# One recurrence unit takes its second read-back from another ring of buffers, and the last attention unit prepares its last queries and gates at later steps

## The chip, the cores and the metric

The kernel runs on one core of one Trainium2 chip. The core has several engines that run side by side, each with its own queue of instructions: TensorE (PE in the profile) multiplies matrices, ScalarE (ACT) and VectorE (DVE) work element by element, GpSimd (POOL) does little here, and SyncE (SP) issues the transfers between the chip's memory and the buffers of the core. An engine works its queue from the front: an instruction that waits holds up what stands behind it. The metric is the time of one execution on the device in microseconds.

## The reference

The reference is one layer of an encoder over 2048 tokens of width 1024, in 32-bit floats. The tokens form a grid of 32 rows by 64 columns.

```python
mod = c_act @ ada_w[l] + ada_b[l]
shift, scale, gate = jnp.split(mod, 3, axis=-1)
h = (_layernorm(x) * (1.0 + scale[:, None, :]) + shift[:, None, :]).astype(x.dtype)
proj = h @ w_in[l]
q_h, i_h, zf_fw, zf_bw, g_h, q_n, k_n, v_n, g_n = jnp.split(proj, split_pts, axis=-1)
y_hg = _hgrn2_branch(q_h, i_h, zf_fw, zf_bw, g_h, lb_fw_all[l], lb_bw_all[l], hg_norm_g[l])
o_na = _neighbourhood_attention(na_heads(q_n), na_heads(k_n), na_heads(v_n), rpb[l])
...
y_na = o_na * jax.nn.silu(g_n)
y = jnp.concatenate([y_hg, y_na], axis=-1) @ w_out[l]
z = DEEPNORM_ALPHA * x + gate[:, None, :] * y
x = (_layernorm(z) * ln_g[l] + ln_b[l]).astype(x.dtype)
```

One projection of 1024 to 9216 columns feeds two branches. The first is a gated linear recurrence with 8 heads of 128, run forwards and backwards over the sequence in chunks of 32; the two directions are added, normalised by their root mean square and multiplied by a gate. The second is a neighbourhood attention with 16 heads of 64: each query sees a window of 8 rows by 16 columns around it, with a bias by relative position, and its output too is multiplied by a gate. Both outputs, 2048 columns together, go through one output projection, and the residual and a layer norm end the layer.

## The kernel before

Each product of 32-bit floats is made from three faster ones: an operand is split into a high part (a rounded copy, made on ACT) and a low part (what is left, a subtraction on DVE), and PE multiplies high by high, high by low and low by high. In the names, h and l at the end mark the parts: `wh` and `wl` of weights that come in as `wr`, `qh` and `ql`, `KA`/`KB` and `KL`, `yh` and `yl`.

The work goes in phases. The start makes the modulation, the normalised `h`, and the first projections, and runs the attention of the first half of the rows. Then come 16 units of the recurrence, 8 heads (`u` = 0 to 7) for the first half of the tokens and 8 for the second, woven with projection matmuls (the helper at L278, which the profile shows as `pj<-h,wh`). A border follows, in which the last recurrence unit drains while PE works on the value projection (`vproj`, L291, with the evacuation of its PSUM tiles on ACT at L299 and the store at L301). Then 8 units of neighbourhood attention for the second half, woven with further projections; the last of them is woven with the first 4 of 16 token tiles of the output projection (`out_stream`, matmuls at L1547 to L1549). A dense phase does the rest of the output projection.

PE runs its instructions in the order in which the program writes them. The orders of ACT, DVE, POOL and SP are set by a scheduler that simulates a timeline: what is ready earlier by its model, or has priority, comes first. A change in the program's text can so move an instruction on these engines, or leave it where it was.

Buffers are rings: `tl(tag)` takes the next buffer of the ring `tag`, and whoever writes it waits until the last reader of the tile that had it is done. Four rings matter here. `cl` has 4 buffers of 128 by 512 floats and `de` has 2 (both belong to the recurrence phase); `bk` has 4, and `vt` holds outputs and raw weights, both in the attention phase. Memory of a phase that has ended is used again by the next: the attention's tile `Z`, which POOL clears at L771 and L772, lies over buffers of the recurrence.

Of a recurrence unit of the second half, the function `hgrn_tail` (L622) does the end. The forward state of the first half goes into the second by three matmuls (L690) on the queries `qh` and `ql`, which were stored earlier and are read back (L683, L684), and their result is added (L691) to a partial output `o1`, read back at L685; `sg`, read back at L686, is the gate. This is done for two groups `g` of 512 tokens, one after the other. `rms_out` (L342) then squares on ACT (L345), splits on DVE (L347, L349), sums over the channels on PE (L354, L355), takes the root on ACT (L357, L358), multiplies on DVE (L359, and by the gate L361), and stores (L362). All four tiles of each group come from `cl`, so that the second group's tiles take the first group's buffers.

In the attention phase `Prep` makes what a unit's steps read: `k` and `q` split keys and queries (keys: ACT L992, DVE L994; queries: ACT L976 and L977, DVE L978 and L979), `gate` makes a gate tile (ACT L1010, L340, L341, DVE L339, L1012), `v` loads values, `table` loads biases. `prep_now` (L1140) says at which of a unit's steps these are written in the program. A step's scores go from PE (L1055 to L1062) to DVE (L1071, bias and row maximum), ACT (L1076, exponential), DVE (L1080 and L1081, division by the sum), PE (L1104, transposes), ACT or DVE (L1110, L1108, copies), and PE (L1126, times the values); DVE then multiplies by the gate (L1136). In the last unit `wo_load` (L1499) and `wo_split` (L1504) bring in and split weights of the output projection (load L1502, high part on ACT L1507, low part on DVE L1508), by steps written in a table `extra`, and `y_split` splits the inputs (ACT L1539, DVE L1540).

Of the kernel before, what the change touches and what calls it, by code (L numbers as in the profile page):

```python
# [11 lines left out]
F32R = mybir.dt.float32r  # L12
# [26 lines left out]
def body(ctx: ExitStack, tc: tile.TileContext, t):  # L39
# [48 lines left out]
    def nm(s):  # L88
        cnt[0] += 1
        return f"{s}_{cnt[0]}"  # L90

    def tl(tag, dt=F32, shape=None):
        if tag in cur["smap"]:
            tag = cur["smap"][tag]
            return sh.tile([P, 512], dt, tag=tag, name=nm(tag), bufs=SH[tag])
        return cur["pool"].tile([P, 512] if shape is None else shape, dt, tag=tag, name=nm(tag), bufs=cur["bufs"].get(tag, 1))
# [536 lines left out]
    def hgrn_tail(u, half, sgs, ubs, decs, qibs, os_, decb_all):  # L633
# [8 lines left out]
        for g in (1, 0):  # L642
# [20 lines left out]
            if half == 0:  # L663
                dma(op_d[u][:, tk], ob)
                dma(sg_d[u][:, tk], sgs[g])
                qb, qh, ql = tl("t"), tl("cl", F32R), tl("cl", F32R)
# [9 lines left out]
        if half == 1:  # L676
            Rh, Rl = tl("Sb", F32R, [P, P]), tl("Sb", F32R, [P, P])
            dve.tensor_copy(Rh, R)
            dve.tensor_tensor(Rl, R, Rh, op=ALU.subtract)
            for g in range(2):  # L680
                tk = slice(g * 512, (g + 1) * 512)
                qh, ql, o1, sg = tl("cl", F32R), tl("cl", F32R), tl("cl"), tl("cl")
                dma(qh.bitcast(F32), qb_d[u][:, 0, tk])  # L683
                dma(ql.bitcast(F32), qb_d[u][:, 1, tk])  # L684
                dma(o1, op_d[u][:, tk])  # L685
                dma(sg, sg_d[u][:, tk])  # L686
                yield
                po = ps("pc")
                for i, (a, b) in enumerate(((Rh, qh), (Rh, ql), (Rl, qh))):
                    pe.matmul(po, a, b, start=i == 0, stop=i == 2)  # L690
                dve.tensor_tensor(o1, po, o1, op=ALU.add)  # L691
                yield from rms_out(u, g, o1, sg, g * 512)
# [445 lines left out]


    def prep_now(st):  # L1140
        return {0: [(st.k, 3), (st.k, 4)], 1: [(st.q, 3), (st.gate, 2)], 2: [(st.v, 7), (st.v, 5), (st.v, 6)], 4: [(st.gate, 3), (st.table, "bot", 0)],
                6: [(st.table, "bot", 1)], 7: [(st.table, "bot", 3)]}

# [314 lines left out]
    with psum_phase("n0", NPS), tc.manual_schedule(engines={mybir.EngineType.PE}):  # L1458
        with phase("st", SB_, SMS), tc.manual_schedule(engines={getattr(mybir.EngineType, e) for e in ("PE", "SP", "Activation", "DVE")}):
            raws, feed, first = startup()  # L1460
        with phase("n0", NB0, SM0):
            natten_init(4, 0)
            st = first_half(raws, feed, first)
# [7 lines left out]
    with psum_phase("h", *HPS), phase("h", HB, SMH), tc.manual_schedule(engines={mybir.EngineType.PE}):  # L1471
        hgrn_init()
        tail = iter(())
        for i in range(16):
            half, u = divmod(i, 8)
            if i < 15:
                nxt = hgrn_dense((i + 1) % 8, (i + 1) // 8, i in (6, 7), reload if i == 6 else None)
                tail, st = weave(hgrn(u, half, st, tail), nxt, HTOT, HSUM)
# [133 lines left out]
    with psum_phase("n1", NPS), phase("n1", NB1, SM1), tc.manual_schedule(engines={mybir.EngineType.PE}):  # L1612
        natten_init(4, 1)
        st = st0
# [13 lines left out]
        for u in range(8):  # L1628
# [15 lines left out]
            st = nxt  # L1644
# [77 lines left out]
```

## Time and profile before

| what | value |
|---|---|
| runs | 2594.27, 2596.82, 2599.92 us (median 2596.82) |
| profiled execution | 2596.31 us, of which 2594.5 us from the first to the last instruction |
| mean granted TensorE clock | 0.995 of full speed |
| busy: PE, DVE, ACT, POOL | 2557.3, 1752.1, 1438.9, 108.5 us |
| the border, 1600 to 1760 us: PE busy | 157.72 of 160.00 us |
| attention of the second half, 1760 to 2290 us: PE busy | 522.43 of 530.00 us |
| dense end, 2290 to 2594.5 us: PE busy | 295.56 of 304.50 us (instructions' modelled ends) |

Times in a profile count from the first instruction. A row of the timeline has the start, the length, the engine, the line, what is written and read, how many instructions it stands for and, in brackets, the idle time before it and what ended that. Matmuls follow each other faster than one lasts, since they overlap in the array; so the spacing of a block of them tells their cost, not the length of one. "SPq" rows are issues of transfers: the length is the time that the queue spends on the issue, not the transfer. The granted clock is the share of its full rate that TensorE was given in a stretch.

### The profile page before, as it was taken

What the parts mean: (1) busy time and instruction counts of PE and PEld (TensorE: products, weight loads), DVE (VectorE), ACT (ScalarE), POOL (GpSimd) and SP (SyncE); (2) the same over time, 40 slices, a digit from 0 to 9 for tenths busy, and PEclk for the clock granted to TensorE, in tenths of its full rate; (3) what the DMA queues carried; (4) which work ended last, traced back from release to release, by engine and by line L of the source; (5) the groups of instructions that cost most, each with busy time, mean ns of one, the idle gap of its engine ahead of it and who ended that gap; (6) DMA issues with size and microseconds to landing.
All of it is one profiled execution on the core that took longest, in us unless ns stands there. A gap on an engine that the chain in (4) does not pass through costs nothing.

```text
span 2594.5 us, 46029 instructions
## 1 busy us (share of the span) xinstructions
PE 2557.3 (99%) x17196; PEld 2154.2 (83%) x17196; DVE 1752.1 (68%) x4394; ACT 1438.9 (55%) x2869; POOL 108.5 (4%) x143
## 2 busy tenths in 40 slices
PE   8999999999999999999999999999999999999998
PEld 6888888878888888888888888898888887788887
DVE  7445545387877778877888787555777778648443
ACT  5533444376666666666766666455777777531110
POOL 0000000000000000000000000000000000032221
PEclk9999999999999999999999999999999999999999
DMA  7566454212122226222222222345455556443331
GB/s 293 143 206 154 143 178 140 90 51 70 66 73 74 66 85 228 83 73 86 80 65 69 82 86 83 120 128 155 123 145 136 147 139 173 132 155 130 96 95 57
DMA packets 230527, 304.79 MB, mean 117 GB/s; under 512 B 29351, under 2 KB 118055, under 8 KB 229159
## 3 DMA queue, kind: packets, MB, share of 16 engines
q1 hardware_dynamic: 230303, 301.85, 37.9%
q8 instruction: 135, 2.21, 0.4%
q14 instruction: 89, 0.73, 0.1%
HBM read 222.37 MB, written 71.18 MB: 113 GB/s over the span
## 4 chain that ended last, share of the span: by engine, by line
PE 94%; DVE 3%; ACT 1%; DMA 1%; issue 0%; SPq 0%; DVEq 0%; ACTq 0%
PE pj L278 51%; PE pj L291 7%; PE ps L1549 4%; PE ps L1547 4%; PE ps L1548 4%; PE ps L1126 3%; PE ps L1104 3%; PE ps L482 2%; PE ps L474 2%; PE ps L1055 2%; PE ps L549 1%; PE ps L278 1%; PE ps L578 1%; PE ps L1062 1%; PE ps L580 1%; PE ps L521 1%
## 5 line engine op out<-in xcount | busy, mean ns | idle before, releaser
L278 PE MATMUL pj<-h,wh 128*128 128x512 f32 x3984 | 1264.7, 398 | 1.5 <-ACT wh L814 1.1
L278 PEld LDWEIGHTS pj<-h,wh 128*128 128x128 f32 x3984 | 721.8, 188 | 149.8 <-issue 10.5
L278 PE MATMUL pj<-h,wl 128*128 128x512 f32 x1992 | 780.3, 392 | 0.0
L278 PEld LDWEIGHTS pj<-h,wl 128*128 128x128 f32 x1992 | 373.8, 188 | 82.4 <-DVE wl L815 0.4
L1076 ACT ACTIVATE pbuf<-pbuf,mx 128x480 f32<-128x480 f32 (+5 forms) x256 | 152.5, 597 | 107.5 <-DVE mx L1071 106.4
L291 PE MATMUL pj<-wh,h 128*128 128x256 f32 x1024 | 197.1, 287 | 2.2 <-ACT vt L299 2.0
L1071 DVE CUSTOM_DVE_ANT_1 pbuf<-ps,bias 128x480 f32<-128x480 f32 (+5 forms) x256 | 129.1, 540 | 98.8 <-PE ps L1062 42.1
L291 PEld LDWEIGHTS pj<-wh,h 128*128 128x128 f32 x1024 | 164.6, 193 | 6.0 <-ACT vt L299 3.3
L269 DVE TENSOR_TENSOR wl<-wr,wh 128x512 fp32r<-128x512 f32 x192 | 131.4, 685 | 46.2 <-ACT wh L268 45.9
L268 ACT ACTIVATE wh<-wr 128x512 fp32r<-128x512 f32 x192 | 120.3, 626 | 73.1 <-PE pj L278 66.7
L291 PE MATMUL pj<-wl,h 128*128 128x256 f32 x512 | 145.6, 284 | 0.0
L1110 ACT ACTIVATE pt<-ps 120x384 f32<-120x384 f32 (+3 forms) x128 | 65.2, 510 | 120.1 <-PE ps L1104 119.9
L1104 PE MATMUL ps<-ident,pbuf 128*128 128x128 f32 (+2 forms) x832 | 112.9, 273 | 4.7 <-DVE pbuf L1081 3.9
L1108 DVE COPY pt<-ps 120x384 f32<-120x384 f32 (+3 forms) x128 | 74.9, 585 | 62.5 <-PE ps L1104 61.6
L1104 PEld LDWEIGHTS ps<-ident,pbuf 128*128 128x128 f32 (+2 forms) x832 | 96.6, 136 | 22.7 <-ACT pbuf L1076 2.5
L468 DVE TENSOR_TENSOR de<-e,de 128x512 f32<-128x512 f32 x64 | 44.2, 691 | 92.9 <-ACT de L467 92.9
L1523 ACT ACTIVATE yh<-yr 128x512 fp32r<-128x512 f32 x52 | 32.7, 628 | 132.4 <-PE ps L1548 115.2
L1596 DVE TENSOR_TENSOR vt<-ps,gt 128x512 f32<-128x512 f32 x24 | 16.5, 692 | 129.9 <-PE ps L1549 129.9
L1081 DVE TENSOR_SCALAR pbuf<-pbuf,mx 128x480 f32<-128x480 f32 (+5 forms) x256 | 101.0, 412 | 3.7
L788 ACT ACTIVATE e<-pj 128x512 f32<-128x512 f32 x97 | 57.8, 596 | 78.9 <-PE pj L278 72.0
L291 PEld LDWEIGHTS pj<-wl,h 128*128 128x128 f32 x512 | 98.8, 193 | 1.0
L840 DVE TENSOR_TENSOR wl<-wr,wh 128x512 fp32r<-128x512 f32 x68 | 46.9, 691 | 69.4 <-ACT wh L839 64.3
(289 smaller groups left out, 4771.2 us busy)
## 6 DMA issues: line engine op xcount, KB each, us to landing
wr<-in_w_in SPq DMA_DIRECT2D x276, 256.0 KB
yr<-yq SPq DMA_DIRECT2D x64, 256.0 KB
bias<-tint SPq DMA_DIRECT2D x24, 480.0 KB
x<-in_x SPq DMA_DIRECT2D x32, 256.0 KB
ada<-in_ada_m SPq DMA_DIRECT2D x8, 1024.0 KB
wr<-in_w_v SPq DMA_DIRECT2D x32, 256.0 KB
nv<-vt SPq DMA_DIRECT2D x32, 256.0 KB
hs<-s SPq DMA_DIRECT2D x32, 256.0 KB
```

The source lines that it names most:

```text
L268: act.activation(hi, raw, AF.Copy)
L269: dve.tensor_tensor(lo, raw, hi, op=ALU.subtract)
L278: pe.matmul(pz, a, b, start=(k == 0 and n == 0), stop=(k == KT - 1 and n == 2))
L291: pe.matmul(pzs[tp][:, i * 256:(i + 1) * 256], a, b, start=(k == 0 and n == 0 and i == 0), stop=(k == KT - 1 and n == 2), skip_group_check ...
L1071: return dve.tensor_tensor_reduce(s[:, 0:nk].rearrange("p (r c) -> p r c", c=kw), sc[:, 0:nk].rearrange("p (r c) -> p r c", c=kw), bt[:, 0 ...
L1076: act.activation(s[:, 0:nk], s[:, 0:nk], AF.Exp, scale=-1.0, bias=mx[:, 0:1], accum_out=mx[:, 1:2])
L1081: dve.tensor_scalar(s[:, 0:nk], s[:, 0:nk], mx[:, 2:3], 1.0, op0=ALU.mult, op1=ALU.mult)
L1104: pe.transpose(ptp[0:cw, c * P:(c + 1) * P], s[:, c * cw:(c + 1) * cw], ident)
L1126: pe.matmul(self.po[R][hs_, j * P:(j + 1) * P], v[:, hh * 64:hh * 64 + 64], pts[hh][0:n * KW[j], c * P:(c + 1) * P], start=(c == 0), stop= ...
L1547: pe.matmul(pz, yh[:, kk], wh, start=first, stop=False)
L1548: pe.matmul(pz, yh[:, kk], wl, start=False, stop=False)
L1549: pe.matmul(pz, yl[:, kk], wh, start=False, stop=last)
```

## The change

The first part gives `o1` and `sg` of one group of one unit (the second group of unit 7, the last of the recurrence) buffers of the ring `de` in place of `cl`. The second writes, for the last attention unit (`st.p == 7`) alone, `q(3)` at step 5 in place of 1, `gate(2)` at step 3 in place of 1, and `gate(3)` at step 6 in place of 4, and leaves the other entries where they were.

```diff
             dve.tensor_tensor(Rl, R, Rh, op=ALU.subtract)
             for g in range(2):
                 tk = slice(g * 512, (g + 1) * 512)
-                qh, ql, o1, sg = tl("cl", F32R), tl("cl", F32R), tl("cl"), tl("cl")
+                qh, ql = tl("cl", F32R), tl("cl", F32R)
+                o1, sg = (tl("de" if u == 7 and g else "cl") for _ in range(2))
                 dma(qh.bitcast(F32), qb_d[u][:, 0, tk])
                 dma(ql.bitcast(F32), qb_d[u][:, 1, tk])
                 dma(o1, op_d[u][:, tk])
@@ -1138,6 +1139,9 @@
 
 
     def prep_now(st):
+        if st.p == 7:
+            return {0: [(st.k, 3), (st.k, 4)], 2: [(st.v, 7), (st.v, 5), (st.v, 6)], 3: [(st.gate, 2)], 4: [(st.table, "bot", 0)], 5: [(st.q, 3)],
+                    6: [(st.gate, 3), (st.table, "bot", 1)], 7: [(st.table, "bot", 3)]}
         return {0: [(st.k, 3), (st.k, 4)], 1: [(st.q, 3), (st.gate, 2)], 2: [(st.v, 7), (st.v, 5), (st.v, 6)], 4: [(st.gate, 3), (st.table, "bot", 0)],
                 6: [(st.table, "bot", 1)], 7: [(st.table, "bot", 3)]}
```

From L684 on, line numbers of the changed kernel are higher by 1, and after `prep_now` by 4: the addition at L691 is L692, the split at L1507 is L1511.

On SP, in the border of before, the read-backs of the second group of unit 7 (tiles numbered 18763 to 18766) stand in this row, with loads of value weights between them:

```order
L683 DMA cl_3598_18763<-qb7 128x512
L684 DMA cl_3599_18764<-qb7 128x512
L262 DMA wr_3659_19208<-in_w_v 128x512
L262 DMA wr_3662_19214<-in_w_v 128x512
L685 DMA cl_3600_18765<-op7 128x512
L362 DMA yq1<-t_3597_18760 128x512
L686 DMA cl_3601_18766<-sgd7 128x512
```

In the changed kernel the second group's `o1` and `sg` (18765 and 18766) stand here, ahead of `o1` and `sg` of the first group (18686 and 18687), whose two query tiles are the rows ahead:

```order
L684 DMA cl_3585_18684<-qb7 128x512
L685 DMA cl_3586_18685<-qb7 128x512
L686 DMA de_3600_18765<-op7 128x512
L687 DMA de_3601_18766<-sgd7 128x512
L686 DMA cl_3587_18686<-op7 128x512
L362 DMA yq1<-t_3517_18289 128x512
L687 DMA cl_3588_18687<-sgd7 128x512
```

So two read-backs moved ahead by some fifteen rows; the two query tiles of the second group, still in `cl`, stayed where they were.

On DVE, before, the addition to the second group's `o1` (L691) stands behind the split of a value weight (L269):

```order
L359 TENSOR_TENSOR t_3596_18756<-t_3596_18756,cl_3587_18686 128x512
L361 TENSOR_TENSOR t_3597_18760<-t_3596_18756,cl_3588_18687 128x512
L269 TENSOR_TENSOR wl_3635_18933<-wr_3633_18930,wh_3634_18932 128x512
L691 TENSOR_TENSOR cl_3600_18765<-ps_3602_18795,cl_3600_18765 128x512
L347 CAST rh_3604_18802<-t_3603_18800 128x512
L349 TENSOR_TENSOR rl_3605_18804<-t_3603_18800,rh_3604_18802 128x512
```

Now:

```order
L359 TENSOR_TENSOR t_3596_18756<-t_3596_18756,cl_3587_18686 128x512
L361 TENSOR_TENSOR t_3597_18760<-t_3596_18756,cl_3588_18687 128x512
L692 TENSOR_TENSOR de_3600_18765<-ps_3602_18795,de_3600_18765 128x512
L269 TENSOR_TENSOR wl_3635_18933<-wr_3633_18930,wh_3634_18932 128x512
L347 CAST rh_3604_18802<-t_3603_18800 128x512
L349 TENSOR_TENSOR rl_3605_18804<-t_3603_18800,rh_3604_18802 128x512
```

The addition has moved ahead of one split. On PE the two sums of `rms_out` (L354 and L355) that stood three and some twenty matmuls into the next block of the value projection now stand at its start and six matmuls into it.

On ACT, a little later in the border, two copies fill the tile `Z` (L780; L781 in the changed kernel) and two evacuations (L299) empty a pair of PSUM tiles of the value projection. Before:

```order
L977 ACTIVATE Q_3620_18890<-bk_3369_17547 64x512
L299 ACTIVATE vt_3641_19040<-pj_3639_18942 128x512
L780 ACTIVATE Z_3618_18868<-Q_3619_18889 64x512
L299 ACTIVATE vt_3642_19043<-pj_3640_18943 128x512
L976 ACTIVATE Q_3643_19046<-e_3477_18125 64x512
L977 ACTIVATE Q_3644_19047<-e_3477_18125 64x512
L1010 ACTIVATE sg_3645_19052<-bk_3372_17553 128x512
L780 ACTIVATE Z_3618_18868<-Q_3620_18890 64x512
```

Now:

```order
L978 ACTIVATE Q_3620_18890<-bk_3369_17547 64x512
L781 ACTIVATE Z_3618_18868<-Q_3619_18889 64x512
L781 ACTIVATE Z_3618_18868<-Q_3620_18890 64x512
L299 ACTIVATE vt_3641_19040<-pj_3639_18942 128x512
L299 ACTIVATE vt_3642_19043<-pj_3640_18943 128x512
L977 ACTIVATE Q_3643_19046<-e_3477_18125 64x512
L978 ACTIVATE Q_3644_19047<-e_3477_18125 64x512
L1011 ACTIVATE sg_3645_19052<-bk_3372_17553 128x512
```

Both copies now stand ahead of both evacuations.

In the last attention unit, on ACT, the gate and query rows of the three moved entries stand in the places that they had (the row of `sg` with L341 here is the last of one of them). What moved are two splits of output weights. Before, the tiles read from `vt` come first:

```order
L341 ACTIVATE sg_4860_25080<-sg_4860_25080 128x512
L1507 ACTIVATE wo_4861_25086<-vt_4816_24871 128x512
L1110 ACTIVATE pt_4844_24983<-ps_4843_24979 96x384
L1507 ACTIVATE wo_4863_25090<-vt_4817_24873 128x512
L341 ACTIVATE sg_4919_25312<-sg_4919_25312 128x512
L1076 ACTIVATE pbuf_3613_18861,mx_4849_25016<-pbuf_3613_18861,mx_4849_25016 128x480
L1076 ACTIVATE pbuf_3614_18863,mx_4850_25021<-pbuf_3614_18863,mx_4850_25021 128x480
L788 ACTIVATE e_4852_25050<-pj_4840_24963 128x512
L1110 ACTIVATE pt_4857_25066<-ps_4856_25062 120x384
L780 ACTIVATE Z_3618_18868<-Q_4753_24634 64x512
L780 ACTIVATE Z_3618_18868<-Q_4754_24635 64x512
L1076 ACTIVATE pbuf_3611_18857,mx_4869_25104<-pbuf_3611_18857,mx_4869_25104 128x480
```

Now two tiles read from `bk`, which stood 21 rows further back, take their place:

```order
L341 ACTIVATE sg_4898_25238<-sg_4898_25238 128x512
L1511 ACTIVATE wo_4899_25244<-bk_4862_25082 128x512
L1111 ACTIVATE pt_4844_24983<-ps_4843_24979 96x384
L1511 ACTIVATE wo_4901_25248<-bk_4863_25084 128x512
L341 ACTIVATE sg_4939_25432<-sg_4939_25432 128x512
L1077 ACTIVATE pbuf_3613_18861,mx_4849_25016<-pbuf_3613_18861,mx_4849_25016 128x480
L1077 ACTIVATE pbuf_3614_18863,mx_4850_25021<-pbuf_3614_18863,mx_4850_25021 128x480
L789 ACTIVATE e_4852_25050<-pj_4840_24963 128x512
L1111 ACTIVATE pt_4857_25066<-ps_4856_25062 120x384
L1511 ACTIVATE wo_4858_25074<-vt_4816_24871 128x512
L1511 ACTIVATE wo_4860_25078<-vt_4817_24873 128x512
L781 ACTIVATE Z_3618_18868<-Q_4753_24634 64x512
```

The two from `vt` stand eight rows later, ahead of the copies into `Z`, and the two from `bk` are gone from their old place further back. DVE's low parts (L1508; L1512) moved in the same way.

## The prediction

> **What bounds the kernel now.** I read the busy shares first, then the chain that ended last by engine, then the waits of PE, because the first two leave one question only: where does PE stand still.
>
> ```profile
> PE 2557.3 (99%) x17196; PEld 2154.2 (83%) x17196; DVE 1752.1 (68%) x4394; ACT 1438.9 (55%) x2869; POOL 108.5 (4%) x143
> PE 94%; DVE 3%; ACT 1%; DMA 1%; issue 0%; SPq 0%; DVEq 0%; ACTq 0%
> ```
>
> PE is busy 99% of the span and carries 94% of the chain. The change removes no matmul, so it can pay only where PE waits, or where PE runs at a lower clock. The waits, in us in total, times, and the longest:
>
> ```profile
> PE ps L1104 <- DVE pbuf L1081: 3.9, 2, 2.1
> PE pj L291 <- ACT vt L299: 2.0, 2, 1.8
> ```
>
> Two of these lie where the diff works: L291, in the border where the last recurrence unit drains, and L1104, in the late attention. The chain there, in order of time (start, length, what):
>
> ```profile
> 1710.55 2.77 PE pj L291 x23
> 1713.34 0.70 DVE cl L691
> ...
> 1716.08 3.89 PE pj L291 x20
> ```
>
> The chain leaves PE once, for the addition of L691, the very instruction that reads `o1`. Timeline rows around it, first SP, then DVE, ACT and PE:
>
> ```profile
> 1709.20 0.33 SPq L685 DMA_DIRECT2D cl<-op  x1
> ```
> ```profile
> 1703.70 0.69 DVE L691 TENSOR_TENSOR cl<-ps,cl 128x512 f32<-128x512 f32 x1 [0.71 <-PE ps L690]
> 1710.56 0.69 DVE L269 TENSOR_TENSOR wl<-wr,wh 128x512 fp32r<-128x512 f32 x1 [0.66 <-ACT wh L268]
> 1713.34 0.69 DVE L691 TENSOR_TENSOR cl<-ps,cl 128x512 f32<-128x512 f32 x1 [2.08 <-PE pj L291]
> 1722.35 0.69 DVE L361 TENSOR_TENSOR t<-t,cl 128x512 f32<-128x512 f32 x1
> ```
> ```profile
> 1714.06 0.63 ACT L345 ACTIVATE t<-cl 128x512 f32<-128x512 f32 x1 [3.54 <-DVE cl L691]
> 1714.60 1.07 ACT L299 ACTIVATE vt<-pj 128x512 f32<-128x512 f32 x2
> ```
> ```profile
> 1709.69 0.86 PE L690 MATMUL ps<-cl,Sb 128*128 128x512 f32 x3
> 1713.14 0.28 PE L291 MATMUL pj<-wh,h 128*128 128x256 f32 x1
> 1715.23 0.38 PE L291 MATMUL pj<-wh,h 128*128 128x256 f32 x1 [1.81 <-ACT vt L299]
> ```
>
> Read from the end: PE waits 1.81 us for an evacuation (L299). Its operands were complete at 1713.42 (1713.14 + 0.28), but in ACT's queue it stands behind the square (L345), which waits for L691. L691's product was done at 1710.55 (1709.69 + 0.86), and DVE stood idle 2.08 us. The row lays this on a matmul, but the wait view lays L691's waits on the transfer:
>
> ```profile
> DVE cl L691 <- DMA cl<-op: 18.5, 6, 3.3
> ```
>
> That fits: `o1` was issued only at 1709.20, since its buffer in `cl` is one that the first group used until then, and L691 began 4.1 us later. So a late read-back holds DVE, then ACT, then PE.
>
> The pause has a second cost. Busy time by windows (length, PE busy, PEld, DVE, ACT, POOL, granted clock, DMA share, GB/s):
>
> ```profile
> 1712.60:1716.00 3.40, 1.59 (x12) 1.35 (x12) 1.81 (x3) 1.94 (x4) 0.00 (x0) 1.00 0.49 158
> 1716.00:1719.40 3.40, 3.40 (x18) 3.40 (x17) 0.69 (x1) 0.18 (x1) 0.00 (x0) 0.50 0.73 212
> ...
> 2176.80:2180.20 3.40, 1.93 (x11) 1.31 (x9) 3.34 (x10) 3.25 (x9) 0.00 (x0) 1.00 0.41 123
> 2180.20:2183.60 3.40, 2.76 (x16) 2.22 (x16) 3.36 (x12) 3.12 (x9) 0.00 (x0) 1.00 0.83 247
> 2200.70:2204.10 3.40, 1.22 (x9) 0.77 (x8) 3.37 (x16) 3.40 (x9) 0.00 (x0) 1.00 0.87 182
> 2204.10:2207.50 3.40, 3.40 (x10) 2.63 (x9) 3.12 (x6) 2.42 (x5) 0.00 (x0) 0.50 1.04 267
> ```
>
> After the window with 1.59 of 3.40 us busy the clock is 0.50 for one window; so it is after 1.22. After 1.93 it stays at 1.00. The threshold lies between 1.59 and 1.93 of a window.
>
> **The change part by part: the border.** Three terms.
>
> First, the wait. `o1` and `sg` of the second group now go into `de`, whose last readers are the transposes of the same unit:
>
> ```profile
> 1664.65 0.60 PE L474 MATMUL ps<-ident,de 128*128 128x128 f32 x4
> ```
> ```profile
> 1666.22 0.32 SPq L685 DMA_DIRECT2D cl<-op  x1
> ```
>
> The buffers are free at 1665.25, and the two issues go ahead of the one that stood at 1666.22, some 43 us earlier than 1709.20. SP stood still there until 1666.22 anyway, so the waits on the transposes are covered; the two issues themselves delay the first group's `o1` by about 0.7 us (two of 0.33), and its reader is the L691 at 1703.70, more than 30 us away. Without that cover SP would lose about 1 us there, and nothing behind it is due so soon. With the data there, L691 can start at 1710.6 and end at 1711.3, the square ends at 1711.9, L269, then L347 and L349, follow behind on DVE, and ACT is free well before the pair's matmuls end at 1713.4. The first PSUM tile of the pair is complete six matmuls earlier, at 1712.7 by the spacing of 0.12 (2.77 / 23), so its evacuation ends at about 1713.3, and PE goes on. Gain between 1.6 (an evacuation that still sticks out by 0.2) and 1.81; I take 1.8.
>
> Second, the other wait of the same row (2.0 in total less 1.8): 0.2 us for an evacuation behind a copy into `Z`. Both copies now go ahead of both evacuations. Gain between 0 and 0.2; I take 0.2. Their price, should they come late, is the rival below.
>
> Third, the clock. Twenty matmuls took 3.89 us in the slow window; at 0.12 they take 2.4. Gain 1.5; at most half a window, 1.7; at least 0, if the same window is slow for another cause or another pause takes its place. I take 1.5, since both ends of it are measured on the same matmuls. [...] Whether a pause halves a window also depends on how it lies across the grid of windows. For 1.81 us to fall whole into one of 3.40, the chance is (3.40 - 1.81) / 3.40 = 0.47; where 1.47 (3.40 - 1.93) were nearly enough it is 0.67. So of other executions of before perhaps 6 in 10 pay these 1.5 us, if the grid isn't tied to the start. [...]
>
> **The last attention unit.** Written later, but the rows of `q(3)`, `gate(2)` and `gate(3)` stay where they were on ACT and DVE. So the waits there stay:
>
> ```profile
> 2180.84 0.84 PE L1104 MATMUL ps<-ident,pbuf 128*120 128x128 f32 x6 [2.12 <-DVE pbuf L1081]
> 2202.70 0.50 PE L1104 MATMUL ps<-ident,pbuf 128*96 128x128 f32 x3 [1.74 <-DVE pbuf L1081]
> 2203.65 0.51 PE L1104 MATMUL ps<-ident,pbuf 128*96 128x128 f32 x3 [0.45 <-DVE mx L1080]
> ...
> 2220.00 0.39 PE L1547 MATMUL pj<-wo,yh 128*128 128x512 f32 x1
> ```
>
> What moves is a split of weights:
>
> ```profile
> 2208.72 0.63 ACT L1507 ACTIVATE wo<-vt 128x512 fp32r<-128x512 f32 x1 [2.20 <-DMA vt<-in_w_out]
> ...
> 2213.61 0.49 ACT L1110 ACTIVATE pt<-ps 120x384 f32<-120x384 f32 x1 [0.74 <-PE ps L1104]
> ```
>
> ACT waited 2.20 us for weights in `vt`. In their place come two tiles that were loaded long before. But this wait lies behind the gaps at 2202.70 and 2203.65, and in the list of PE's waits no line names a split of these weights: the gain is 0, covered by PE's own matmuls. The cost side: the `vt` splits now follow the copy at 2213.61. Two of 0.63 on ACT end near 2215.4, the low parts on DVE near 2216, and the first matmul that reads them is that at 2220.00: 4 us to spare. The scores on DVE behind them move by what two low parts take, 1.4 us by the row of L269; their transposes stand behind the matmul at 2220.00 in PE's order. Cost 0. The ends for this part: a gain of 2.2 (1.74 + 0.45) and half a window at most, 1.7, together 3.9, if the two gaps close; a loss of some 1 us, if the splits are later by 5 us than worked out.
>
> **Sum.** 1.8 + 0.2 + 1.5 + 0 = 3.5 us off the profiled execution, 2596.31 to 2592.8. The profiled execution is 0.5 us under the median of the runs (2596.82), so against that the forecast is 2593.3. All after the border shifts by 3.5, almost exactly one window of 3.40, so in an execution with the same grid the later gaps keep their place in it. 0.2% is 5.2 us, about what a measurement of this kernel can tell from no change: bounds 2591.6 and 2602.0. The forecast is a gain, but inside them.
>
> **The rivals.** The first: the late read-back goes and PE closes up, but the window of 0.50 near 1716 has another cause than the pause and stays, so that only the two waits are gained: 2593.3 + 1.5 = 2594.8. Against it stand both windows of 0.50, each directly behind one with under 1.6 us busy. [...]
>
> The second: the last unit pays too. Should ACT and DVE, with other work in their place, reach the division (L1081) in time, 2.2 us and up to 1.7 of clock go as well: 2593.3 - 3.9 = 2589.4, faster. For it: ACT and DVE are busy 3.40 and 3.37 of 3.40 us in the window of that gap, so any row that left would help. Against it: none left ahead of 2208.
>
> The third, on the other side: the copies into `Z`. Since `Z` lies over the ring `de`, POOL may clear it only when the gate product L361 of the second group has read `sg`; before, it could much earlier:
>
> ```profile
> 1690.17 0.52 POOL L772 MEMSET Z<- 64x512 f32 x1
> ```
> ```profile
> 1728.26 0.60 ACT L299 ACTIVATE vt<-pj 128x512 f32<-128x512 f32 x1 [2.43 <-PE pj L291]
> 1728.88 0.63 ACT L780 ACTIVATE Z<-Q 64x512 fp32r<-64x512 f32 x1
> 1729.42 0.57 ACT L299 ACTIVATE vt<-pj 128x512 f32<-128x512 f32 x1
> ```
>
> ACT takes its queue in order, so both evacuations now wait for two memsets (1.04) and two copies (1.26). If L361 ends at T, the second evacuation ends near T + 3.5 (with 1.2 for two evacuations). PE needs it at about 1726.5, 3.5 before its old end of 1730. I expect T near 1717.5: PE's two sums end near 1714.5, and two steps on ACT (0.63 each, as the square) and two on DVE (0.69 each) follow. That leaves 5 us. Even at its old end, 1723.04, T + 3.5 = 1726.5 costs nothing. It decides from T = 1730: then 3.5 us are lost and the gain is gone. At 1733 the loss is 6.5 and a slow window 1.5, so 4.5 net: 2601.3. Nothing in the queues makes L361 so late.
>
> The fourth: phase. Where the grid falls otherwise, another remaining pause (2.12 us at 2180.84) is followed by a slow window: 1.5 back, 2594.8. The fifth: nothing moves, since another wait follows in the border at once: 2596.8.
>
> **How the numbers follow.** The forecast has 0.60, the first rival 0.07, the second 0.12, the third 0.04, the fourth 0.11, the fifth 0.06. Faster by over 0.2% are the second and a tenth of the forecast, by the scatter of the runs (2594.27 to 2599.92): 0.18. Slower by over 0.2%: the third in part, and scatter on the fifth, 0.04. The rest, 0.78, is within 0.2%. The range goes from the second rival, 2589.4, to 2597.5, the fifth with some scatter; it leaves out the third and what scatter puts beyond the second. Without the rivals the forecast's own range is 2592 to 2595.
>
> **What the changed profile would show.** Read-backs `de<-op` and `de<-sgd` issued near 1666; the addition (now L692) directly behind its matmuls near 1710.6, with no wait on the transfer; the waits of L291 on L299 gone or under 0.3; no window of 0.50 near 1716; the root (L357) near 1715 and not 1720; the gaps of 2.1, 1.7 and 0.4 still there near 2177 and 2199, with their slow window; no wait of 2.2 for `vt` on ACT. I am wrong if L299 still ends a wait of PE, if copies into `Z` hold ACT past the pair's end, if the late gaps close, or if the end of the span moves by other than 2 to 4 us.

## The result and the profile after

Eight runs of the changed kernel have a median of 2591.84 us (2586.60 to 2594.80), eight of the kernel before, on the same chip, 2597.62 us (2593.74 to 2601.97). The ratio is 0.9976, with a 95% interval of 0.9965 to 0.9987. So the change gains 0.24%, or some 6 us, with 3 to 9 in the interval. The profiled execution took 2592.41 us with a span of 2590.6, 3.9 us below the one of before.

The page of the kernel after, busy time and chain:

```profile
PE 2555.5 (99%) x17196; PEld 2152.1 (83%) x17196; DVE 1752.1 (68%) x4394; ACT 1439.0 (56%) x2869; POOL 108.5 (4%) x143
PE 93%; DVE 3%; DMA 2%; ACT 1%; issue 0%; SPq 0%; DVEq 0%
```

PE is the bound as before. What the border looks like now, first the read-backs on SP, then DVE, POOL and ACT (lines of the changed kernel are higher by one):

```profile
1660.20 0.34 SPq L686 DMA_DIRECT2D de<-op  x1
1665.23 0.32 SPq L687 DMA_DIRECT2D de<-sgd  x1
1666.11 0.33 SPq L686 DMA_DIRECT2D cl<-op  x1
```
```profile
1710.49 0.69 DVE L692 TENSOR_TENSOR de<-ps,de 128x512 f32<-128x512 f32 x1 [0.69 <-PE ps L691]
...
1716.65 0.69 DVE L361 TENSOR_TENSOR t<-t,de 128x512 f32<-128x512 f32 x1
```
```profile
1717.62 0.53 POOL L772 MEMSET Z<- 64x512 f32 x1 [37.63 <-ACT KA L993]
1718.20 0.52 POOL L773 MEMSET Z<- 64x512 f32 x1
```
```profile
1712.64 1.32 ACT L299 ACTIVATE vt<-pj 128x512 f32<-128x512 f32 x2 [0.80 <-PE pj L291]
...
1720.17 1.29 ACT L781 ACTIVATE Z<-Q 64x512 fp32r<-64x512 f32 x2
1724.62 1.31 ACT L299 ACTIVATE vt<-pj 128x512 f32<-128x512 f32 x2 [3.17 <-PE pj L291]
```

`o1` is issued at 1660.20, 49 us earlier than before. The addition follows its matmuls at once, 2.85 us earlier than before; the evacuations come when PE is done with their tiles and not behind a late square. The chain of the same stretch has only PE left in it:

```profile
1713.32 0.23 PE ps L354
1713.55 0.72 PE pj L291 x6
1714.27 0.23 PE ps L355
1714.50 16.79 PE pj L291 x138
```

138 matmuls in 16.79 us are 0.122 each, through the place where 20 took 3.89 us before. The windows there, and those around the late pause (columns as in the prediction, the granted clock third from the end):

```profile
1712.80:1716.20 3.40, 3.40 (x29) 3.30 (x28) 1.20 (x3) 3.19 (x6) 0.00 (x0) 1.00 0.74 229
1716.20:1719.60 3.40, 3.40 (x30) 3.40 (x30) 3.17 (x6) 3.23 (x8) 1.04 (x2) 1.00 0.49 159
2197.10:2200.50 3.40, 1.21 (x7) 0.58 (x7) 3.37 (x15) 3.40 (x10) 0.00 (x0) 0.97 0.39 110
2200.50:2203.90 3.40, 3.40 (x11) 2.77 (x10) 3.12 (x7) 3.40 (x8) 0.00 (x0) 0.53 1.01 177
```

The border runs at full clock. The late pause and its slow window are still there; PE's rows in the last attention unit:

```profile
2177.44 0.84 PE L1105 MATMUL ps<-ident,pbuf 128*120 128x128 f32 x6 [1.68 <-DVE pbuf L1082]
2199.30 0.50 PE L1105 MATMUL ps<-ident,pbuf 128*96 128x128 f32 x3 [1.74 <-DVE pbuf L1082]
2200.25 0.84 PE L1105 MATMUL ps<-ident,pbuf 128*96 128x128 f32 x3 [0.45 <-DVE mx L1081]
```

The profile alone thus shows the border's 3.7 us (1.81 and 0.16 of waits, and 1.7 for one window at half clock) and 0.4 us less at 2177. That leaves about 2 us between the medians to be explained, and the question whether the second part of the change does anything.

### The profile page after: what moved, and what is told of

It is laid out like the page before. It is cut to its first block, busy times and chain, and to the rows that moved or that the text cites. A ratio compares the mean times of both kernels' runs of the same rounds, so it can differ in the third digit from the quotient of the medians.

```text
span 2590.6 us, 46031 instructions
## 1 busy us (share of the span) xinstructions
PE 2555.5 (99%) x17196; PEld 2152.1 (83%) x17196; DVE 1752.1 (68%) x4394; ACT 1439.0 (56%) x2869; POOL 108.5 (4%) x143
## 4 chain that ended last, share of the span: by engine, by line
PE 93%; DVE 3%; DMA 2%; ACT 1%; issue 0%; SPq 0%; DVEq 0%
PE pj L278 51%; PE pj L291 7%; PE ps L1551 4%; PE ps L1552 4%; PE ps L1553 4%; PE ps L1127 3%; PE ps L1105 3%; PE ps L482 2%; PE ps L474 2%; PE ps L1056 2%; PE ps L549 1%; PE ps L578 1%; PE ps L1063 1%; PE ps L580 1%; PE ps L521 1%; PE ps L659 1%
## 5 line engine op out<-in xcount | busy, mean ns | idle before, releaser
L291 PE MATMUL pj<-wh,h 128*128 128x256 f32 x1024 | 195.2, 285 | 0.3 <-ACT e L789 0.3
L291 PEld LDWEIGHTS pj<-wh,h 128*128 128x128 f32 x1024 | 163.0, 191 | 3.7 <-ACT vt L299 0.9
L269 DVE TENSOR_TENSOR wl<-wr,wh 128x512 fp32r<-128x512 f32 x192 | 131.4, 685 | 46.5 <-ACT wh L268 44.2
L268 ACT ACTIVATE wh<-wr 128x512 fp32r<-128x512 f32 x192 | 120.2, 626 | 73.0 <-PE pj L278 66.6
L291 PE MATMUL pj<-wl,h 128*128 128x256 f32 x512 | 144.7, 283 | 0.0
L291 PEld LDWEIGHTS pj<-wl,h 128*128 128x128 f32 x512 | 98.0, 191 | 1.0
```

The lines of the kernel that those rows point to most:

```text
L268: act.activation(hi, raw, AF.Copy)
L269: dve.tensor_tensor(lo, raw, hi, op=ALU.subtract)
L291: pe.matmul(pzs[tp][:, i * 256:(i + 1) * 256], a, b, start=(k == 0 and n == 0 and i == 0), stop=(k == KT - 1 and n == 2), skip_group_check ...
```

## The experiments

The theory to test first was the one of the prediction: the border carries everything. Its rival: the last attention unit pays too, in a way that the two profiles don't show. The parts were run alone. Each ratio below is against the kernel before on the same chip; its median there lay between 2596.78 and 2597.11 us.

### The ring alone

```diff
-                qh, ql, o1, sg = tl("cl", F32R), tl("cl", F32R), tl("cl"), tl("cl")
+                qh, ql = tl("cl", F32R), tl("cl", F32R)
+                o1, sg = (tl("de" if u == 7 and g else "cl") for _ in range(2))
```

> The kernel before with the change of rings alone. If the border carries the whole gain, the span falls by 3.9 us as in the profile of the changed kernel (2594.5 to 2590.6): no pause of 1.8 us at L291, no window at half clock near 1716, and the waits of the last attention unit of 2.1, 1.7 and 0.4 us stay as before. If the last attention unit pays for the rest of the 5.8 us between the medians, this kernel gains about 2 us less than the changed one.

Measured: median 2593.59 us, ratio 0.9987 (0.9979 to 0.9996).

### The later preparation alone

```diff
+        if st.p == 7:
+            return {0: [(st.k, 3), (st.k, 4)], 2: [(st.v, 7), (st.v, 5), (st.v, 6)], 3: [(st.gate, 2)], 4: [(st.table, "bot", 0)], 5: [(st.q, 3)],
+                    6: [(st.gate, 3), (st.table, "bot", 1)], 7: [(st.table, "bot", 3)]}
```

> The kernel before with the later preparation in the last attention unit alone. If the border carries the whole gain: no difference from before, 0 within 1 us of the profiled span once windows at half clock are counted, the pause of 1.8 us at 1715 is there, and the only thing gone is the wait of 2.2 us of ACT for weights in vt near 2208. If the last unit pays: about 2 us faster than before, with shorter waits of L1104 near 2180 or 2202.

Measured: median 2593.40 us, ratio 0.9986 (0.9977 to 0.9995), though the profiled execution, one of the slower ones of this kernel, has the span of before, 2594.4 us.

### The changed kernel again

> The changed kernel once more beside the two parts. If the parts do not touch each other, its gain is the sum of those of e1_ring and e2_prep, 3.5 to 4 us; if the 5.8 us of the medians are real and not the scatter of the runs, it is 5 to 7 us.

Measured: median 2591.08 us, ratio 0.9976 (0.9966 to 0.9986), which is about the sum of the two parts (0.0013 and 0.0014). So the border does not carry everything; by the ratios each part has about half. The profiles say in part how. This is the kernel with the ring alone, ACT and then PE behind the late pause:

```profile
2205.95 0.63 ACT L1508 ACTIVATE wo<-vt 128x512 fp32r<-128x512 f32 x1 [3.87 <-DMA vt<-in_w_out]
2206.49 0.47 ACT L1111 ACTIVATE pt<-ps 96x384 f32<-96x384 f32 x1
```
```profile
2199.20 0.50 PE L1105 MATMUL ps<-ident,pbuf 128*96 128x128 f32 x3 [0.44 <-DVE mx L1081]
...
2207.01 0.32 PE L1127 MATMUL ps<-pt,V 96*64 96x128 f32 x1 [3.36 <-ACT pt L1111]
```
```profile
2200.40:2203.80 3.40, 3.25 (x24) 2.18 (x23) 2.50 (x4) 1.68 (x4) 0.00 (x0) 1.00 1.04 198
2203.80:2207.20 3.40, 0.19 (x4) 0.19 (x6) 1.59 (x5) 1.25 (x3) 0.00 (x0) 1.00 0.74 229
2207.20:2210.60 3.40, 3.40 (x16) 2.58 (x14) 2.86 (x10) 2.15 (x6) 0.00 (x0) 0.56 0.89 203
```

ACT waits 3.87 us for the weights in `vt`, the copy `pt` stands behind that in its queue, and PE waits 3.36 us for the copy, and pays a slow window on top. It is the wait of ACT that the prediction quoted at 2.20 us and priced at 0. In the profile of before the copy and its matmuls stand in these rows, where the third of the three matmuls waited 0.09 us:

```profile
2209.26 0.47 ACT L1110 ACTIVATE pt<-ps 96x384 f32<-96x384 f32 x1
```
```profile
2209.30 0.80 PE L1126 MATMUL ps<-pt,V 96*64 96x128 f32 x3
```

Two things made it look free. There the window from 2204.1 to 2207.5 ran at half clock, so that PE came to this place 6.0 us after its transposes (2203.65 to 2209.7) and not 4.5 us after (2199.20 to 2203.65); and the copy came 5.6 us after them (2209.26) and not 7.3 (2206.49). 1.6 us of slow PE and 1.7 us of an earlier transfer hid 3.3 us. In the second profile of the changed kernel, where this stretch ran at full clock, no such wait of PE is left.

### `o1` alone in the other ring

```diff
-                qh, ql, o1, sg = tl("cl", F32R), tl("cl", F32R), tl("cl"), tl("cl")
+                qh, ql = tl("cl", F32R), tl("cl", F32R)
+                o1, sg = tl("de" if u == 7 and g else "cl"), tl("cl")
```

> The kernel before with o1 alone in the ring de, sg still in cl. L691 reads only o1, so if its late arrival is what held DVE, ACT and PE, the gain is the same 3.5 to 4 us. If the second read-back matters too, the gate product L361 waits for sg: issued near 1709.5 and there about 4 us later, near 1714, against a use at 1716.6, so at most its own 0.7 us should be lost, and no pause of PE.

Measured: median 2593.43 us, ratio 0.9985 (0.9976 to 0.9995), the same as with both read-backs moved, and L291 no longer waits for L299 in the border. The late `o1` is what held the border; where `sg` comes from does not matter. The late wait is here as well, with full clock ahead of it:

```profile
2205.91 0.32 PE L1127 MATMUL ps<-pt,V 96*64 96x128 f32 x1 [2.42 <-ACT pt L1111]
```

### The kernel before, once more

> The kernel before, one more profiled execution. If the wait of ACT for weights in vt near 2208 is one whose cost to PE depends on when the transfer lands and on whether a window at half clock slows PE ahead of it, then here the wait of L1126 for the copy L1110 near 2209 is 1.5 to 3.5 us where PE ran at full clock from 2204 on, and under 0.3 where that window was slow again. If the 0.09 us of the first profile are the rule, it is under 0.3 in either case.

Measured: 2594.49 us, span 2592.7. Again a slow window (2203 to 2206) ran ahead of this place, and again PE lost only 0.23 us there while ACT waited 2.31. So the cover by the slow window is seen twice, and its absence in the two kernels with a change of ring and no later preparation. No profile of the unchanged kernel without that window was seen; that it would lose 1.5 us or more there is worked out, not shown.

The same execution shows that the slow window does not always follow a pause. Here is the border, with a pause as long as in the first profile, and two windows laid on the grid on which this execution's slow windows fall:

```profile
1712.97 0.38 PE L291 MATMUL pj<-wh,h 128*128 128x256 f32 x1 [1.86 <-ACT vt L299]
```
```profile
1711.18:1714.59 3.41, 1.62 (x12) 1.57 (x13) 2.34 (x4) 2.12 (x4) 0.00 (x0) 1.00 0.52 169
1714.59:1718.00 3.41, 3.41 (x30) 3.37 (x29) 0.19 (x2) 1.48 (x3) 0.00 (x0) 1.00 0.55 157
```

The first window holds nearly the whole pause, with PE busy for 1.62 us, and the next is at full clock; in the first profile 1.59 us were followed by half clock. In the kernel with the later preparation alone the pause was 1.85 us, and a window at half clock followed, as in the first profile.

### The pause put back

```diff
                 dve.tensor_tensor(o1, po, o1, op=ALU.add)
+                for _ in range(5 if u == 7 and g else 0):
+                    dve.tensor_scalar(o1, o1, 1.0, 1.0, op0=ALU.mult, op1=ALU.mult)
```

> The changed kernel with five extra multiplications by one on DVE behind the addition to o1 of the second group, so that the data is there early but the square on ACT is late. If the pause at L291 is what the ring took away, this puts it back: PE waits 1.6 to 2.0 us for L299 near 1715, and the time is 2 us above that of the changed kernel, or 3.7 where a window at half clock follows. If the gain of the ring came from somewhere else (the transfers, the order on SP), the time stays within 1 us of the changed kernel.

Measured: median 2595.02 us, ratio to before 0.9991 (0.9982 to 0.9999), 3.2 to 3.9 us above the two medians of the changed kernel, though the intervals of the ratios overlap a little. The read-back is early (issued at 1657.69), and still PE stands; the window is again one of the grid:

```profile
1712.57 0.38 PE L291 MATMUL pj<-wh,h 128*128 128x256 f32 x1 [1.85 <-ACT vt L299]
```
```profile
1713.15:1716.56 3.41, 3.41 (x18) 3.31 (x17) 0.07 (x1) 0.00 (x0) 0.00 (x0) 0.50 0.73 228
```

So it is the pause that costs, with its slow window, and not the transfer or the order on SP. Two things delay the square here, and they end together: the last multiplication at 1711.37, and a split of value weights (L268) that the scheduler put ahead of the square, at 1711.39. The pause is the same, 1.85 us. Not all of this profile's distance to the changed kernel is the border's: PE also waited 3.14 us at 2180, where the two profiles of the changed kernel have 1.68 and 1.30.

### The preparation held to its written place

The written order of the second part had no effect on the rows of `q(3)` and the gates. Here they are held in program order on ACT.

```diff
-            keep = pinned if raw is self.bk.get("q") or self.first else lambda x: x
+            keep = pinned if raw is self.bk.get("q") or self.first or (self.p == 7 and R == 3) else lambda x: x
...
+            late = self.half == 1 and self.p == 7 and R in (2, 3)
+            keep = pinned if raw is self.bk.get("g") or self.first or late else lambda x: x
```

> The changed kernel with q(3), gate(2) and gate(3) of the last unit held to their written places on ACT, so that their rows really leave the stretch before 2203. If ACT and DVE were too full there, the waits of L1105 near 2199 of 1.74 and 0.45 us go and with them the window at half clock that can follow: 2 to 4 us faster than the changed kernel. If something else ends last there, the waits stay and the time is the same within 1 us.

Measured: median 2592.07 us, ratio to before 0.9979 (0.9971 to 0.9988): the same as the changed kernel. The waits near 2199 went, as they should if ACT and DVE were too full there, but there are others, of which those behind 2217 are new:

```profile
2177.35 0.84 PE L1106 MATMUL ps<-ident,pbuf 128*120 128x128 f32 x6 [3.10 <-DVE pbuf L1083]
2197.77 0.83 PE L1106 MATMUL ps<-ident,pbuf 128*96 128x128 f32 x6 [0.30 <-DVE pbuf L1083]
2217.26 0.50 PE L1553 MATMUL pj<-wo,yh 128*128 128x512 f32 x1 [0.22 <-DVE wo L1513]
2223.13 0.51 PE L1552 MATMUL pj<-wo,yh 128*128 128x512 f32 x1 [1.54 <-ACT wo L1512]
2223.94 0.50 PE L1553 MATMUL pj<-wo,yh 128*128 128x512 f32 x1 [0.30 <-DVE wo L1513]
```

### An earlier wait for weights: one split later

PE's wait near 2177 differs from profile to profile with a wait of ACT for a transfer into `vt` some 6 us ahead of it:

| kernel | ACT waits for `vt` | PE waits near 2177 |
|---|---|---|
| before | 1.89 | 2.12 |
| after | 1.44 | 1.68 |
| ring alone | 0.77 | 1.30 |
| later preparation alone | 3.30 | 3.53 |
| `o1` alone | 2.52 | 2.75 |

```diff
-                    extra = {4: [(wo_load, 0, 0, 1)], 5: [(wo_load, 0, 2, 3, 4, 5)], 7: [(wo_split, 0, 0, 1)], 8: [(wo_split, 0, 2, 3), (wo_load, 0, 6, 7)],
-                             9: [(y_early, 0, 1), (wo_split, 0, 4, 5)], 10: [(y_split, 0), (wo_split, 0, 6, 7), (wo_load, 1, 0, 1, 4, 5)]}
+                    extra = {4: [(wo_load, 0, 0, 1)], 5: [(wo_load, 0, 2, 3, 4, 5)], 7: [(wo_split, 0, 0, 1)], 8: [(wo_load, 0, 6, 7)],
+                             9: [(wo_split, 0, 2, 3), (y_early, 0, 1), (wo_split, 0, 4, 5)], 10: [(y_split, 0), (wo_split, 0, 6, 7), (wo_load, 1, 0, 1, 4, 5)]}
```

> The changed kernel with the split of output weights 2 and 3 of the first column half written one step later (step 9 in place of 8 of the unit before the last). The waits of L1105 near 2177 were 2.12, 1.68, 1.30, 3.53 and 2.76 us in five profiles, where ACT waited 1.89, 1.44, 0.77, 3.30 us and more for a transfer into vt near 2172. If that transfer is the cause, the wait near 2177 falls under 0.5 us and the time by 1.5 to 3 us. If the work on ACT and DVE is the cause, the wait stays over 1 us.

Measured: median 2594.74 us, ratio to before 0.9990 (0.9981 to 0.9999), 3 us slower than the changed kernel. The wait at 2177 is gone altogether with the split that waited for the transfer. As the work of the split left the place too, this run alone does not say which of the two it was. The scheduler also moved other rows on DVE, and PE waits 1.89 us at 2142, 4.25 at 2200 and 2.16 at 2219 instead.

### Other rings for the weights, three ways

The first has the ring change alone and no later preparation; weights 0 and 1 of the second half come through `bk` (`wr3` in the code), 6 and 7 through `vt` (`wr`):

```diff
-            wraws[k, n] = tl("wr2" if k in (4, 5) else "wr3" if (k, n) in ((6, 1), (7, 1)) else "wr")
+            wraws[k, n] = tl("wr2" if k in (4, 5) else "wr3" if (k, n) in ((0, 1), (1, 1)) else "wr")
```

> The kernel of e1_ring (no later preparation), with the rings of four loads of output weights changed about: weights 0 and 1 of the second column half come through bk, which is free early, and weights 6 and 7 through vt. All splits, queries and gates stay in the places of e1_ring. If the late transfer into vt is what made PE wait 3.36 us in e1_ring and 2.43 in e4_o1_only, that wait of L1127 is gone and the time is that of the changed kernel, near 2591.5. If the later queries and gates are what the changed kernel gains by, the time stays at that of e1_ring, near 2593.5.

Measured: median 2595.42 us, ratio 0.9993 (0.9984 to 1.0002). The wait of L1127 is gone with the late transfer taken away, all splits and gates in place: the transfer was its cause. But the gain did not come, since the next weights through `vt` are late instead:

```profile
2225.23 0.63 ACT L1508 ACTIVATE wo<-vt 128x512 fp32r<-128x512 f32 x1 [4.67 <-DMA vt<-in_w_out]
```
```profile
2225.91 0.79 PE L1548 MATMUL pj<-wo,yh 128*128 128x512 f32 x1 [3.85 <-ACT wo L1508]
```

The second and third bring weight 3 of the first half and weight 0 of the second through `bk`, with the preparation held in place and without:

```diff
-            wraws[k, n] = tl("wr2" if k in (4, 5) else "wr3" if (k, n) in ((6, 1), (7, 1)) else "wr")
+            wraws[k, n] = tl("wr2" if k in (4, 5) else "wr3" if (k, n) in ((3, 0), (0, 1)) else "wr")
```

> The kernel of e7_pinned_prep with weight 3 of the first half and weight 0 of the second loaded through bk, and weights 6 and 7 of the second half through vt. In e7 the waits near 2199 fell from 2.2 to 0.3 us, but 3.1 us stayed near 2177 behind a transfer, and 2.1 us of waits for split weights came up from 2217 to 2224. If both come from transfers into vt that land late, the wait near 2177 falls under 0.5 us and those near 2220 under 1 us, and the time is 3 to 5 us below the changed kernel, near 2587.5. If the ring only passes the lateness on to the next weights, other waits of 2 us or more come up further on, and the time is within 1.5 us of the changed kernel.

Measured: median 2594.80 us, ratio 0.9993 (0.9984 to 1.0002). The wait near 2177 is 1.30 us with no wait of ACT for a transfer ahead of it, so what stood above 1.3 in the table was the transfer, and 1.3 is left to other work on ACT and DVE. PE waits 4.68 us at 2222.9 for the split of a weight that came late into `vt`.

> The changed kernel with the same change of rings as e10_pinned_early, but without holding q and the gates. The wait near 2177 (1.3 to 3.5 us in seven profiles) falls under 0.5 us if the transfer of weight 3 is its cause; the waits near 2199 of 1.74 and 0.45 us stay. Time 1.5 to 3 us below the changed kernel, near 2589.5; within 1 us of it if the lateness passes on.

Measured: median 2605.04 us, ratio 1.0032 (1.0020 to 1.0045), slower than before. The wait near 2177 is 1.30 us here too, as it should be. But the splits whose transfers into `vt` come last now stand ahead of other rows in ACT's queue, and all of it stood behind them:

```profile
2229.30 1.22 ACT L1511 ACTIVATE wo<-vt 128x512 fp32r<-128x512 f32 x2 [14.98 <-DMA vt<-in_w_out]
```
```profile
2231.06 1.97 PE L1127 MATMUL ps<-pt,V 128*64 128x128 f32 x14 [13.08 <-ACT pt L1111]
```

In all three the lateness was passed on: what was in time by one ring was late by the other.

### Held in place, and the weights that are there first

```diff
-                extra = {0: [(wo_load, 1, 2, 3)], 1: [(wo_split, 1, 0, 1), (wo_load, 1, 6, 7)], 2: [(wo_split, 1, 2, 3, 4, 5)], 3: [(wo_split, 1, 6, 7)]}
+                extra = {0: [(wo_load, 1, 2, 3)], 1: [(wo_split, 1, 0, 1), (wo_load, 1, 6, 7)], 2: [(wo_split, 1, 6, 7), (wo_split, 1, 2, 3, 4, 5)]}
```

> The kernel of e7_pinned_prep with the splits of weights 6 and 7 of the second half, which are in bk long before, written ahead of those of 2 to 5, so that ACT does them while it waits for vt. In e7 PE waited 1.54 and 0.30 us near 2223 for these splits. If that is all that stood in the way, these waits go, the waits near 2199 stay at 0.3 us, and the sum of PE's waits falls from 27.8 to about 26 us: the time is 1 to 3 us below the changed kernel (2591.1 to 2591.8), near 2589.5. If the lateness passes on again, a wait of over 1 us comes up between 2205 and 2245 and the time is within 1 us of the changed kernel.

Measured: median 2590.43 us (2587.45 to 2591.42), ratio to before 0.9973 (0.9962 to 0.9983). In the profile no wait of PE over half a microsecond stands between 2180 and 2240:

```profile
2174.99 0.84 PE L1106 MATMUL ps<-ident,pbuf 128*120 128x128 f32 x6 [1.92 <-DVE pbuf L1083]
2195.41 0.83 PE L1106 MATMUL ps<-ident,pbuf 128*96 128x128 f32 x6 [0.30 <-DVE pbuf L1083]
2215.22 0.50 PE L1553 MATMUL pj<-wo,yh 128*128 128x512 f32 x1 [0.48 <-DVE wo L1513]
```

It is the lowest median of the study, but its interval and that of the changed kernel overlap nearly in full: a version that is at least as good, not one shown to be better.

### Where the microseconds are

Three numbers explain the spans of the profiled executions: the sum of PE's waits (the idle time ahead of each PE instruction, summed over the timeline), the number of windows of 3.41 us at half clock between 50 us and 2570 us, and a rest.

| kernel | span | PE's waits | slow windows | rest: span - waits - 1.7 each |
|---|---|---|---|---|
| before | 2594.5 | 28.3 | 4 (91, 562, 1716, 2204) | 2559.4 |
| before again | 2592.7 | 27.9 | 3 (561, 2179, 2203) | 2559.7 |
| after | 2590.6 | 26.2 | 3 (91, 562, 2200) | 2559.3 |
| after again | 2584.8 | 24.9 | 0 | 2559.9 |
| ring alone | 2593.2 | 29.1 | 3 (91, 562, 2208) | 2559.0 |
| later preparation alone | 2594.4 | 29.1 | 3 (1713, 2181, 2205) | 2560.2 |
| `o1` alone | 2590.6 | 29.2 | 1 (2174) | 2559.7 |
| pause put back | 2594.8 | 30.2 | 3 (1713, 2181, 2205) | 2559.5 |
| held in place | 2590.1 | 27.8 | 1 (561) | 2560.6 |
| held, weights that are there first | 2585.7 | 24.9 | 1 (560) | 2559.1 |
| one split later | 2595.4 | 29.6 | 4 (2143, 2198 twice running, 2222) | 2559.0 |
| other rings, the first | 2594.3 | 30.9 | 2 (2225 twice running) | 2560.0 |
| other rings, the second | 2591.2 | 29.4 | 2 (561, 2224) | 2558.4 |
| other rings, the third | 2605.1 | 38.6 | 7 (91, 562, 2200, 2221 four times running) | 2554.6 |

In all but the last row the rest is the same within 2.2 us, and the spans differ by 10.6. The last row shows where the count fails: of the four windows from 2221 on PE was busy for 0.00, 0.00, 0.15 and 3.41 us, so three of them slowed nothing; counted with four windows in place of seven, the rest is 2559.7. The two executions of the changed kernel differ by 5.8 us with not one instruction changed, which is 3 slow windows (5.1) and 1.3 of waits, less 0.6 of rest. Their rows of span and clock:

```profile
core 0: 2590.6 us, clock 0.996
```
```profile
core 0: 2584.8 us, clock 0.999
```

## Why the prediction was right or wrong

The time measured, 2591.84 us, lies in the range, 2589.4 to 2597.5, and the sign was right. The single value, 2593.3, was 1.5 us too high, and the gain was put at 3.5 us where the medians show 5.8. By the ratio the gain is 0.24% (0.13 to 0.35), and a gain of over 0.2% had been given a chance of 0.18. The range reached so far down for the second rival, whose mechanism did not come; that the time still lies in it is in part luck.

**The wait in the border (1.8).** Right, with the row by row account: L692 at 1710.49 (1710.6 forecast), the evacuation from 1712.64 (1712.7), the sums' end at 1714.50 (1714.5), the gate product's end at 1717.34 (1717.5), no pause. One row came otherwise, at no cost: `o1` was issued at 1660.20, 5 us before its buffer was thought to be free (1665.25). `o1` alone gave the same gain as the ring alone, and the pause put back took it away.

**The second wait there (0.2).** Right; it was 0.16 us in the trace of before, and no wait of L291 on L299 is left in the border.

**The clock (1.5).** Right in kind: the slow window of the border is gone. In size it is a matter of chance, as said: of four profiled executions with the pause of 1.8 us, a slow window followed in three. The forecast gave 0.47 to 0.67, by the way the pause falls across the grid; but the pause without a slow window lay nearly as whole in its window (1.79 us) as the others. Nor does the threshold between 1.59 and 1.93 us of busy time hold. The trace of before itself has these two windows, the first with 1.95 us busy and the second at half clock:

```profile
87.84:91.25 3.41, 1.95 (x12) 1.39 (x11) 2.96 (x6) 3.17 (x6) 0.00 (x0) 1.00 0.59 158
91.25:94.66 3.41, 3.41 (x11) 2.73 (x10) 0.56 (x1) 1.58 (x3) 0.00 (x0) 0.50 0.43 153
```

Where the term occurs it is 1.7 us, 3.41 us at a clock of 0.50.

**The last attention unit (0).** This is the step that failed: "the gain is 0, covered by PE's own matmuls". The cover was a window at half clock, which the prediction had quoted and not connected with it, and a transfer that happened to land early. Without the window the same wait of ACT cost PE 2.42 and 3.36 us in the two profiles with a change of ring and no later preparation, and with the late transfer taken out of its way that wait was gone. By the ratios the later preparation is worth about 0.0011 to 0.0014, some 3 us. What was right is how it works: the written order of `q(3)` and the gates moved nothing, the waits of 1.74 and 0.45 us stayed, and two splits that were loaded long before took the place of two that ACT had to wait for. One thing stays open: in the kernel before, both profiles have the cover, and the one profile of the later preparation alone shows no gain, so why it gains 3 us there by the medians is not shown.

**The rivals.** The first (the slow window has another cause) is out: with the pause gone no slow window came in the border in ten profiles out of ten, and with the pause put back it came again, in the one profile taken. The second (the late gaps close) did not happen; the gain of the last unit came by another wait. The third (late copies into `Z`) did not: POOL cleared at 1717.62 to 1718.72, ACT came to the copies only at 1720.17, and the evacuation at 1724.62 waited for PE. Its sum has a slip: PE needs the tile at 1726.5, so the loss begins at T = 1726.5 - 3.5 = 1723.0, the whole gain is gone at T = 1726.5 and not at 1730, and T = 1733 would have given 2604.8 and not 2601.3. T came at 1717.34, so nothing hung on it. The fourth (the phase): a slow window behind the pause near 2177 came in the second profile of the kernel before (2179), and the scatter is larger than it was given: not one window more or less, but none to four per execution of the kernels before and after, between 50 and 2570 us.

## What to carry to other kernels

A wait that a profile shows as hidden is only as safe as what hides it: look at the clock in the stretch that gives the cover, and at whether the released time is a transfer's landing, before pricing it at nothing; here the cover was a window at a clock of 0.50 and a transfer that landed early, and in two profiles without that window the wait cost PE 2.42 and 3.36 us. Where an in-order queue waits for a transfer, putting work there whose data came long before can be worth more than the profile of one execution shows (here 3 us by the medians, with the span of before in the one profile), but only if the late one then stands where its user is still far off; three ways of changing the rings here only chose which weights would be late. Before reading a difference of a few microseconds between two profiles, subtract the windows at half clock and see what is left: here 5.1 of the 5.8 us between two executions of one kernel were three such windows.

## What the runs showed of the hardware

All clocks here are the granted clock that the profile gives for a stretch of an execution.

In the border PE paused for 1.81 us in the profile of before, 1.85 with the later preparation alone, 1.85 with the pause put back and 1.86 in the second profile of the kernel before. In the first three a window of 3.41 us at a clock of 0.50 came next, which at half the rate is 1.7 us; in the fourth the clock stayed at 1.00. In the window that holds the pause PE was busy for 1.60 us in the profile of before (1712.58 to 1715.99), 1.56 with the pause put back (1709.74 to 1713.15) and 1.62 in the execution without a slow window (1711.18 to 1714.59).

In the profile of before the four slow windows between 50 and 2570 us begin at 91.25, 562.29, 1715.99 and 2204.10 us and last 3.41 us each. From one to the next it is 471.04, 1153.70 and 488.11 us, which is 138, 338 and 143 times 3.413 us. In the profile of after they begin at 90.82, 561.86 and 2200.26 us, 471.04 and 1638.40 us apart, 138 and 480 times the same. That is the grid spoken of above. Near 91 and 562 us, where the program is the same in both, it lies 0.43 us apart in the two executions. By the table above the window near 91 us is slow in four of the fourteen profiles and the one near 561 in eight.

PE's busy time in a window does not say by itself whether the next is slow. On the grids of the profiles of before and after the slow windows followed 1.95, 0.61, 1.60 and 1.23 us busy in the first and 1.95, 1.12 and 1.22 in the second. In the first 1.93 us (from 2176.80) and 2.08 us (from 57.12) were followed by a clock of 1.00, and so were the 1.62 us of the second profile of the kernel before. So 1.95 us went with half clock and 1.93 with full clock in one and the same execution; what decides was not shown.

Two executions of the changed kernel differ by three slow windows, 5.1 us, nearly the 5.8 us between the medians of the kernels before and after.
